# Slots of the activations' high and low parts that are 32 bytes longer, in a two-layer hybrid decoder trunk on one core

## The chip, the core and the metric

The kernel runs on one core of a Trainium2 chip. The metric is device time in microseconds, of one execution of the whole program; the figure for the kernel before is the median of three runs. The engines named are TensorE (PE, and PEld for its weight loads), VectorE (DVE), ScalarE (ACT), GpSimd (POOL) and SyncE (SP, which here only issues DMAs).

## What is computed

Two layers of a decoder trunk, on 512 tokens of 2,048 features, in float32. In each layer one projection of the normalised input feeds two groups of eight heads: differential attention (group A, two softmax maps per head and a bias by distance) and latent attention (group B, queries and keys by way of compressed latents, with a rotary part). Each group is gated; both are concatenated, projected back and added to x.

```python
for l in range(DEPTH):                       # DEPTH = 2
    h = _rms_norm(x, norm_g[l])              # (1, 512, 2048)
    proj = jnp.einsum('bsd,de->bse', h, w_in[l])
    q_a, k_a, v_a, z_a, c_q, c_kv, k_r, z_b = jnp.split(proj, split_points, axis=-1)
    o_a = _diff_attention(qa, ka, va, lam, rel_bias_table)
    o_a = (_rms_norm(o_a, diff_subln_g[l]) * (1.0 - lambda_init)).reshape(...) * jax.nn.silu(z_a)
    q_b  = _rms_norm(c_q, mla_q_norm_g[l])  @ w_uq[l]
    kv   = _rms_norm(c_kv, mla_kv_norm_g[l]) @ w_ukv[l]
    o_b = _mla_attention(q_nope, q_rope, k_nope, k_rope, v_b).reshape(...) * jax.nn.silu(z_b)
    x = x + jnp.concatenate([o_a, o_b], axis=-1) @ w_out[l]
return _rms_norm(x, final_norm_g)
```

## The kernel before, in words

**Layout.** Everything is kept with features on the 128 partitions and tokens along them: x is 16 chunks of 128 features by 512 tokens. For accuracy each operand is split exactly into two parts, high and low, of a rounded float32 type (float32r), and a product is three matmuls: high weights by high x, high weights by low x, low weights by high x (`mm3`, lines 318 to 321). In these the weights, 128 by 128, are loaded into the array and the 512 columns of x stream past them.

**Slots.** `split_into` (line 256) writes the two parts of chunk k of the scaled input into a slot x0 to x15 of its own, the high part in its first 2,048 bytes of each partition and the low part in the 2,048 after that. ScalarE writes the high part, VectorE the low. In each layer these slots hold the normalised input for the projections; later x0 to x7 hold group B's outputs (`split_mix`, line 924) for the output projection, while group A's outputs lie in slots named mb. In the last layer x8 to x15 hold pairs of the result's chunks (`last_evac`, line 941).

**Weights.** They come as blocks of 128 by 1,024 in the order of use: SyncE loads a block into raw (two slots), ScalarE copies its high part into whi, VectorE subtracts the low part into wlo (lines 94 and 95; two slots each). Loads run two blocks ahead, splits one.

**Jobs.** `job_proj` (line 323) makes 128 features of a projection: 16 chunks by three matmuls. `job_kouter` (line 341) makes the first four at once, chunk by chunk as x arrives. `job_out_half` and `job_out_rest` (lines 457 and 471) make a chunk of the output projection: eight chunks from x0 to x7, then eight from mb. `job_v` (line 412) makes values with tokens on the partitions: here slices of 128 tokens of x (group A) or of the latents in mb (group B) are loaded into the array and 512 columns of whi and wlo stream past (lines 428 to 430). `job_out_tail` (line 505) makes the last two chunks in two halves of 256 tokens. A hand-written schedule (`run_jobs`, line 128, with the tables from line 33 on) puts the attention's scores, transposes and products with the values between the pieces of these jobs, in TensorE's order. SyncE's and GpSimd's orders are written out too; ScalarE's and VectorE's follow the program.

**Where slots begin.** The pool lays the slots one behind the other, in the order of their first use, each rounded up to 32 bytes. In the built program of the kernel before the slots begin at these addresses within a partition, modulo 512 bytes:

| slots, in order of address | begin modulo 512 |
|---|---|
| ones | 128 |
| mb (8 slots of 4,096) | 448 |
| raw, whi, wlo (2 each, of 4,096) | 0 |
| x0, gate, x1, tmp (4), x2 to x7, cs (3), x8 to x15, kr (2) | 0 |
| ma (8), sa (2), v | 96 |
| ptl | 128 |
| pth, sb (2), qa, ka | 160 |

Within a slot, slices of 128 or 512 columns begin at further multiples of 512 bytes. In job_out_first and the tail some blocks of weights lie in v instead of whi and wlo.

Of the kernel before, what the change touches and what calls it, by code (L numbers as in the profile page):

```python
# [10 lines left out]
F32R = mybir.dt.float32r  # L11
# [17 lines left out]
# When the steps of a head's attention come, in pieces (of 6 matmuls) after the  # L29
# head's gate begins: S scores and softmax, T transposes, by blocks of queries; A  # L30
# products with the values, by blocks of keys, and F the norm, after the next
# head's gate begins (for the last head: after its own).
# [4 lines left out]
# When the last head's unit splits the outputs of the first half, and when the norms  # L37
# of the latents come after the units after theirs begin.
# [4 lines left out]
# Chunks of x that are loaded ahead; matmuls that bring the tensor engine's clock up  # L43
# before the first data come.
# [4 lines left out]
# The last chunks of the result come in two parts of the tokens, the first CUT and the rest.  # L49
# [7 lines left out]
def after(at, n):  # L57
    """The times with those of A and F after n more pieces."""
    return {k: tuple(v + n for v in vs) if k == "A" else vs + n if k == "F" else vs for k, vs in at.items()}


class WStream:
    """Weight blocks in the order of their use: loads run ahead, each block is
    split exactly into two float32r parts, hi + lo."""
# [52 lines left out]
def fold(w):  # L117
    """Rows in groups of 128, side by side: (k 128) c -> 128 (k c)."""
    return w.reshape(-1, P, w.shape[1]).transpose(1, 0, 2).reshape(P, -1)


def side_by_side(a, b, k):
    """Columns of k groups each, taken group by group."""
    import numpy as np
    return np.concatenate([a.reshape(P, k, -1), b.reshape(P, k, -1)], axis=2).reshape(P, -1)


def run_jobs(ws, jobs, steps):
    """Pieces of the jobs' matmuls in order; a step (n, f) comes after n pieces."""
    steps = sorted(steps, key=lambda s: s[0])  # L130
    done = s = 0
    for n, gen in jobs:
        for _ in gen():
            done += 1
            n -= 1
            while s < len(steps) and steps[s][0] <= done:
                steps[s][1]()
                s += 1
        assert n == 0
    for _, f in steps[s:]:  # L140
        f()
# [3 lines left out]
def trunk(ctx, tc, blocks, xf, gains, diff_lambda, rel_bias_table, onehot, tables, wb, outf):  # L145
# [25 lines left out]
    # ---------------------------------------------------------------- blocks  # L171
    # Each: its layout from the weights, width, and where its parts go.
# [9 lines left out]
    def b_uq(l, j):  # L182
        """No-position part of head 2j, rope parts of heads 2j and 2j + 1."""
        def block(a):
            w = a["w_uq"][l]
            return side_by_side(fold(w[:, j * 384:j * 384 + 192]), fold(w[:, j * 384 + 320:j * 384 + 384]), 4)
        return block, 1024, "std"

    def b_uk(l, h, with_q):
        """Key part of head h, and the no-position query part when its rope part has been made."""  # L190
        def block(a):
            k = fold(a["w_ukv"][l][:, h * 256:h * 256 + P])
            return side_by_side(k, fold(a["w_uq"][l][:, h * 192:h * 192 + P]), 1) if with_q else k
        return block, 1024 if with_q else 512, "std"

    def b_uv(l, q, j):
        """Value parts of heads 4q to 4q + 3."""
        def block(a):
            w = a["w_ukv"][l][j * 256:(j + 1) * 256, q * 1024:(q + 1) * 1024]
            return fold(w.reshape(256, 4, 256)[:, :, P:].reshape(256, T))  # L200
        return block, 1024, "std"

    # ---------------------------------------------------------------- constants
# [11 lines left out]
    def fetch_x(k, n, eng):  # L215
        """n chunks of x, of 128 features each, in pairs."""
        if k % 2 == 0:
            pair = t_([P, 2, T], F32, "mb", 8)
            xt[k], xt[k + 1] = pair[:, 0, :], pair[:, 1, :]
            dst = pair[:, :n, :]  # L220
        else:
            dst = xt[k].rearrange("p (n t) -> p n t", n=1)
        eng.dma_start(out=dst, in_=xf[k * P:(k + n) * P, :].rearrange("(n p) t -> p n t", p=P))
# [28 lines left out]
    # x, feature-major: hi + lo of x * g; between the layers x itself goes to DRAM for the residual  # L252
# [3 lines left out]
    def split_into(k, src, scale):  # L256
        """hi + lo of src * scale into slot k."""
        both = t_([P, 2, T], F32R, f"x{k}", 1)
        hi, lo = both[:, 0, :], both[:, 1, :]
        if scale is None:  # L260
            nc.scalar.copy(out=hi, in_=src)
            nc.vector.tensor_tensor(out=lo, in0=src, in1=f32(hi), op=ALU.subtract)
        else:
            nc.scalar.activation(out=hi, in_=src, func=AF.Copy, scale=scale)
            nc.vector.scalar_tensor_tensor(out=lo, in0=src, scalar=scale, in1=f32(hi), op0=ALU.mult, op1=ALU.subtract)
        return hi, lo
# [7 lines left out]
    # ---------------------------------------------------------------- RMS  # L274
    def rsqrt_of(dst, src, n):
        """dst = (src / n + eps) ** -0.5: from the logarithm, then a step of Newton's."""
        shape = list(dst.shape)
        u, v = (tmp()[:, :shape[1]], tmp()[:, :shape[1]]) if shape[1] > 4 else [t_(shape, F32, f"rs{i}", 1) for i in range(2)]
        if 4 < shape[1] < T:
            nc.scalar.activation(out=dst, in_=src, func=AF.Ln, scale=1.0 / n, bias=eps[:, 0:1])  # L280
            nc.vector.tensor_scalar(out=u, in0=src, scalar1=1.0 / n, scalar2=EPS, op0=ALU.mult, op1=ALU.add)
        else:
            nc.scalar.activation(out=u, in_=src, func=AF.Identity, scale=1.0 / n, bias=eps[:, 0:1])
            nc.scalar.activation(out=dst, in_=u, func=AF.Ln)
        nc.scalar.activation(out=dst, in_=dst, func=AF.Exp, scale=-0.5)
        nc.scalar.activation(out=v, in_=dst, func=AF.Square)
        nc.vector.scalar_tensor_tensor(out=v, in0=u, scalar=-0.5, in1=v, op0=ALU.mult, op1=ALU.mult)
        nc.vector.scalar_tensor_tensor(out=dst, in0=v, scalar=1.5, in1=dst, op0=ALU.add, op1=ALU.mult)
# [3 lines left out]
    def square_into(src, i, last):  # L292
        """Sum of squares over the chunks, and over partitions after the last."""
# [9 lines left out]
    def ones_sum(acc, tag="kr"):  # L303
        """Sum of acc [P, T] over its partitions, in every partition."""
# [12 lines left out]
    # ---------------------------------------------------------------- jobs  # L317
# [94 lines left out]
    def job_v(blocks, parts, scaled_by):  # L412
        """Values of four heads, token-major: parts(kc) gives the chunk's two parts, features by tokens."""
# [31 lines left out]
    def in_v_slot():  # L445
        """Places for the parts of two blocks, where the values were."""
# [10 lines left out]
    def job_out_half(l, d, accs, ms, dest="std"):  # L457
        """The part of the mixed chunks that come first."""
# [26 lines left out]
    def job_out_first(l, accs, ms, evac, dest):  # L485
        """Rests of the first three chunks; the last mixed chunk comes last."""
# [18 lines left out]
    def job_out_tail(l, ms, evac):  # L505
        """The last two chunks of the result, first for the first part of the tokens."""
# [28 lines left out]
    # ---------------------------------------------------------------- evacuations  # L535
# [5 lines left out]
    def split2(dst, src):  # L541
        """hi + lo of src into dst[:, 0], dst[:, 1]."""
# [77 lines left out]
    def evac_z(acc):  # L620
        """Gate z * sigmoid(z): the reciprocal of 1 + exp(-z) from its logarithm and a step of Newton's."""
# [33 lines left out]
    # ---------------------------------------------------------------- attention  # L655
    PTW = 13 * P

    def softmax(ps, n, bias, scale, tag):
        """exp(s - max) of s = (ps + bias) * scale, and the sum over keys."""
# [136 lines left out]
    # ---------------------------------------------------------------- lambda, bias vectors  # L796
# [25 lines left out]
    def bias_rows():  # L822
        """8 * bias by distance, one row per head, to DRAM."""
# [21 lines left out]
    def stats_x():  # L845
        """1 / rms of x: over all partitions, and with the tokens as partitions."""
# [14 lines left out]
    # ---------------------------------------------------------------- program  # L861
    all_jobs, all_steps = [], []

    def add(jobs, *steps):
        """Jobs, and steps at numbers of pieces after the first job's start."""
# [6 lines left out]
    for l in range(DEPTH):  # L872
# [68 lines left out]
        def last_evac(d, th=None):  # L941
            """A chunk of the result before the last norm, and the sum of squares; all tokens, or a part."""
# [38 lines left out]
        def sums(th):  # L981
            """Sums of squares of all chunks but the last two."""
# [5 lines left out]
        def finish(th):  # L988
            """The final norm of a part of the tokens, and out."""
# [43 lines left out]
# the weights as blocks of [128, 1024] in the order of their use ----  # L1033
# [6 lines left out]
def _shape_constants():  # L1040
    """One-hot T5 buckets by distance, rotary tables, causal mask: of the shapes alone."""
# [49 lines left out]
```

## Time and profile before

| | |
|---|---|
| time, median of 3 runs | 1877.51 us |
| lowest and highest of them | 1877.32 and 1877.66 us |
| span of the profiled execution, first to last instruction | 1874.7 us |
| TensorE busy | 1830.8 us, 98% |
| weight loads (beside the matmuls) | 1482.6 us, 79% |
| VectorE, ScalarE, GpSimd busy | 1001.9, 869.3, 37.9 us |
| matmuls | 8,348 |
| mean granted TensorE clock | 0.990 of full speed |

The device time of the profiled execution itself is not listed apart from its span; what lies around the span is taken as the 2.8 us between it and the median. A row of the order of time gives a start, a duration, engine, line, operation, what is written and read (out<-in, buffer numbers left out), shape and count. The chunk of x is not named in a row; it follows from the order of the matmuls. Matmuls overlap and their recorded ends are modelled, so the distance between two starts is the pace, and the recorded duration (0.39 us for 512 columns) is not. Groups by form give the number of instructions, their busy time and the mean of one.

### The profile page before, as it was taken

Reading aid. Unit: us, or ns where it says so; the run is one execution under the profiler, and the core shown is the slowest. Engines: PE = TensorE matmul, PEld = TensorE weight load, DVE = VectorE, ACT = ScalarE, POOL = GpSimd, SP = SyncE. Lnnn points to the kernel's source line nnn. Section 1 sums busy time; section 2 is a strip of 40 time slices with the busy share of each in tenths; the row PEclk is TensorE's granted clock in tenths of the full one; section 3 lists DMA queues with packets and bytes.
Section 4 is the critical chain, followed back from the end, with each engine's and each line's share of the span. In section 5 each row is a group of like instructions: output and inputs, shape, how many; then the busy total and the mean of one; then the engine's idle time right before and its main releaser. Section 6 shows DMA issues by size and latency. Waiting matters only on the chain.

```text
span 1874.7 us, 21774 instructions
## 1 busy us (share of the span) xinstructions
PE 1830.8 (98%) x8348; PEld 1482.6 (79%) x8348; DVE 1001.9 (53%) x1871; ACT 869.3 (46%) x1532; POOL 37.9 (2%) x74
## 2 busy tenths in 40 slices
PE   9949999999999999999999999999999999999997
PEld 7837778788888888888888877878888888878886
DVE  6616555553666456643445655455456654684334
ACT  6406555442556355622344555454355543663232
POOL 0000000000000000010000000000000000000000
PEclk9979999999999999999999999999999999999999
DMA  6352222233322323244433221222323222233333
GB/s 210 96 83 77 71 68 85 74 90 96 86 83 84 96 93 88 91 135 149 142 120 97 87 74 62 74 79 84 96 85 95 85 85 90 84 85 118 120 116 130
DMA packets 55620, 181.11 MB, mean 97 GB/s; under 512 B 6907, under 2 KB 11003, under 8 KB 55516
## 3 DMA queue, kind: packets, MB, share of 16 engines
q1 hardware_dynamic: 48828, 159.00, 27.3%
q0 software_dynamic: 6400, 20.19, 4.4%
q8 instruction: 66, 1.08, 0.2%
q10 hardware_dynamic: 288, 0.52, 0.1%
q14 instruction: 38, 0.31, 0.1%
HBM read 168.68 MB, written 11.01 MB: 96 GB/s over the span
## 4 chain that ended last, share of the span: by engine, by line
PE 94%; DMA 3%; DVE 2%; ACT 1%; issue 0%; DVEq 0%; ACTq 0%; SPq 0%
PE pacc L319 23%; PE pacc L321 22%; PE pacc L320 22%; PE pacc L428 3%; PE pacc L430 3%; PE pacc L429 3%; DMA raw<-in_blocks_dram 3%; PE ptp L671 2%; PE ps L755 1%; PE po L687 1%; PE po L688 1%; PE po L689 1%; PE ps L320 1%; PE po L430 1%; PE po L429 1%; PE po L428 1%
## 5 line engine op out<-in xcount | busy, mean ns | idle before, releaser
L319 PE MATMUL pacc<-x,whi 128*128 128x512 f32 (+1 forms) x1472 | 590.8, 401 | 11.5 <-ACT whi L94 11.5
L94 ACT CAST whi<-raw 128x1024 fp32r<-128x1024 f32 (+1 forms) x282 | 292.2, 1037 | 642.4 <-PE pacc L320 434.9
L321 PE MATMUL pacc<-x,wlo 128*128 128x512 f32 (+1 forms) x1472 | 575.0, 391 | 0.0
L320 PE MATMUL pacc<-x,whi 128*128 128x512 f32 (+1 forms) x1472 | 574.3, 390 | 0.0
L95 DVE TENSOR_TENSOR wlo<-raw,whi 128x1024 fp32r<-128x1024 f32 (+1 forms) x282 | 340.6, 1208 | 342.4 <-ACT whi L94 338.2
L319 PEld LDWEIGHTS pacc<-x,whi 128*128 128x128 f32 x1472 | 277.4, 188 | 74.8 <-ACT whi L94 11.9
L321 PEld LDWEIGHTS pacc<-x,wlo 128*128 128x128 f32 x1472 | 276.9, 188 | 60.5 <-DVE wlo L95 0.8
L320 PEld LDWEIGHTS pacc<-x,whi 128*128 128x128 f32 x1472 | 277.5, 189 | 50.5
L319 PE MATMUL pacc<-mb,whi 128*128 128x512 f32 (+1 forms) x400 | 159.0, 397 | 0.0
L321 PE MATMUL pacc<-mb,wlo 128*128 128x512 f32 (+1 forms) x400 | 156.2, 391 | 0.6 <-DVE wlo L95 0.6
L320 PE MATMUL pacc<-mb,whi 128*128 128x512 f32 (+1 forms) x400 | 156.2, 390 | 0.0
L664 ACT ACTIVATE sa<-sa,m 128x128 f32<-128x128 f32 (+3 forms) x128 | 71.9, 562 | 127.2 <-DVE m L662 125.4
L662 DVE CUSTOM_DVE_ANT_0 sa<-ps,cs 128x128 f32<-128x128 f32 (+3 forms) x128 | 62.3, 487 | 101.9 <-PE ptp L671 35.6
L539 DVE TENSOR_TENSOR tmp<-pacc,rstd 128x512 f32<-128x512 f32 x64 | 44.0, 688 | 94.9 <-PE pacc L321 94.9
L321 PEld LDWEIGHTS pacc<-mb,wlo 128*128 128x128 f32 x400 | 75.2, 188 | 19.3 <-DVE wlo L95 1.6
L319 PEld LDWEIGHTS pacc<-mb,whi 128*128 128x128 f32 x400 | 75.3, 188 | 16.8 <-issue 0.9
L320 PEld LDWEIGHTS pacc<-mb,whi 128*128 128x128 f32 x400 | 75.4, 188 | 16.2
L677 ACT CAST pth<-ptp 128x128 fp32r<-128x128 f32 (+3 forms) x128 | 53.6, 420 | 64.1 <-PE ptp L671 63.8
L428 PE MATMUL pacc<-whi,x 128*128 128x512 f32 x192 | 76.3, 398 | 0.0
L430 PE MATMUL pacc<-whi,x 128*128 128x512 f32 x192 | 74.9, 390 | 0.0
L429 PE MATMUL pacc<-wlo,x 128*128 128x512 f32 x192 | 74.8, 389 | 0.0
L678 DVE TENSOR_TENSOR ptl<-ptp,pth 128x128 fp32r<-128x128 f32 (+3 forms) x128 | 61.6, 484 | 4.3 <-ACT pth L677 2.4
(248 smaller groups left out, 2332.1 us busy)
## 6 DMA issues: line engine op xcount, KB each, us to landing
raw<-in_blocks_dram SPq DMA_DIRECT2D x282, 512.0 KB, 3.5
cs<-brow POOLq DMA_DIRECT2D x16, 256.0 KB, 3.0
cs<-in_x_dram POOLq DMA_DIRECT2D x16, 256.0 KB, 4.2
cs<-xres POOLq DMA_DIRECT2D x16, 256.0 KB, 2.9
out_dram<-x SPq DMA_DIRECT2D x16, 256.0 KB, 2.2
mb<-in_x_dram SPq DMA_DIRECT2D x7, 512.0 KB, 7.1
brow<-pth POOLq DMA_DIRECT2D x1, 2560.0 KB, 56.7
raw<-in_blocks_dram SPq DMA_DIRECT2D x8, 256.0 KB, 2.6
```

Of the source, the lines that this page charges most:

```text
L94: nc.scalar.copy(out=a[:, :width], in_=r[:, :width])
L95: nc.vector.tensor_tensor(out=b[:, :width], in0=r[:, :width], in1=a[:, :width].bitcast(F32), op=ALU.subtract)
L319: nc.tensor.matmul(acc, wh, rh, start=first, stop=False)
L320: nc.tensor.matmul(acc, wh, rl, start=False, stop=False)
L321: nc.tensor.matmul(acc, wl, rh, start=False, stop=last)
L428: nc.tensor.matmul(accs[t], xhi[:, c], hi[:, w], start=kc == 0, stop=False)
L429: nc.tensor.matmul(accs[t], xhi[:, c], lo[:, w], start=False, stop=False)
L430: nc.tensor.matmul(accs[t], xlo[:, c], hi[:, w], start=False, stop=kc == n - 1)
L662: nc.vector.tensor_tensor_reduce(out=s[:, :n], in0=ps[:, :n], in1=bias, scale=-scale, scalar=3.0e38, op0=ALU.add, op1=ALU.min, accum_out=m ...
L664: nc.scalar.activation(out=s[:, :n], in_=s[:, :n], func=AF.Exp, scale=-1.0, bias=m[:, 0:1], accum_out=m[:, 1:2])
L677: nc.scalar.copy(out=view(h["ph"]), in_=pv)
L678: nc.vector.tensor_tensor(out=view(h["pl"]), in0=pv, in1=f32(view(h["ph"])), op=ALU.subtract)
```

## The change

The slot of chunk k of the scaled input is declared with 8 more elements (32 bytes) per partition than its two parts need. The parts are taken as the first 512 columns and the next 512, so the low part still begins 2,048 bytes after the high part. The other hunks of the diff only take comments away.

```diff
     def split_into(k, src, scale):
-        """hi + lo of src * scale into slot k."""
-        both = t_([P, 2, T], F32R, f"x{k}", 1)
-        hi, lo = both[:, 0, :], both[:, 1, :]
+
+        both = t_([P, 2 * T + 8], F32R, f"x{k}", 1)
+        hi, lo = both[:, 0:T], both[:, T:2 * T]
         if scale is None:
             nc.scalar.copy(out=hi, in_=src)
             nc.vector.tensor_tensor(out=lo, in0=src, in1=f32(hi), op=ALU.subtract)
```

## Rows read from the trace of the kernel before

**Rows 1.** The page, parts 1, 2 and 4: busy time, granted clock, chain.

```profile
PE 1830.8 (98%) x8348; PEld 1482.6 (79%) x8348; DVE 1001.9 (53%) x1871; ACT 869.3 (46%) x1532; POOL 37.9 (2%) x74
...
PEclk9979999999999999999999999999999999999999
...
PE 94%; DMA 3%; DVE 2%; ACT 1%; issue 0%; DVEq 0%; ACTq 0%; SPq 0%
```

**Rows 2.** Waits of TensorE, whole span: total us, times, longest; two longest.

```profile
PE ptp L312 <- ACT sa L307: 15.8, 1, 15.8
PE pacc L319 <- ACT whi L94: 11.5, 1, 11.5
```

**Rows 3.** TensorE in order of time (start us, us), x past weights: 50 matmuls.

```profile
378.81 0.39 PE L319 MATMUL pacc<-x,whi 128*128 128x512 f32 x1
...
389.92 0.39 PE L320 MATMUL pacc<-x,whi 128*128 128x512 f32 x1
```

**Rows 4.** TensorE in order of time, mb past weights: 24 matmuls, then the next.

```profile
846.66 0.39 PE L319 MATMUL pacc<-mb,whi 128*128 128x512 f32 x1
...
852.26 0.39 PE L319 MATMUL pacc<-x,whi 128*128 128x512 f32 x1
```

**Rows 5.** TensorE in order of time, x past weights in v: 24, then the next.

```profile
807.87 0.39 PE L319 MATMUL pacc<-x,v 128*128 128x512 f32 x1
...
813.48 0.39 PE L319 MATMUL pacc<-mb,whi 128*128 128x512 f32 x1
```

**Rows 6.** TensorE in order of time, weights past mb: 28 matmuls.

```profile
285.04 0.39 PE L430 MATMUL pacc<-whi,mb 128*128 128x512 f32 x1
...
291.22 0.40 PE L430 MATMUL pacc<-whi,mb 128*128 128x512 f32 x1
```

**Rows 7.** TensorE's groups by form, within 379:390 (first) and within 846.7:852.2 us.

```profile
L320 PE MATMUL pacc<-x,whi 128*128 128x512 f32 x17 | 6.6, 389 | 0.0
...
L320 PE MATMUL pacc<-mb,whi 128*128 128x512 f32 x8 | 3.2, 394 | 0.0
```

**Rows 8.** TensorE's groups by form, whole span: busy us, mean ns of one.

```profile
L319 PE MATMUL pacc<-x,whi 128*128 128x512 f32 x1456 | 586.3, 403 | 11.5 <-ACT whi L94 11.5
L321 PE MATMUL pacc<-x,wlo 128*128 128x512 f32 x1456 | 570.5, 392 | 0.0
L320 PE MATMUL pacc<-x,whi 128*128 128x512 f32 x1456 | 569.8, 391 | 0.0
...
L321 PE MATMUL pacc<-mb,wlo 128*128 128x512 f32 x384 | 151.8, 395 | 0.6 <-DVE wlo L95 0.6
L320 PE MATMUL pacc<-mb,whi 128*128 128x512 f32 x384 | 151.8, 395 | 0.0
...
L430 PE MATMUL pacc<-whi,x 128*128 128x512 f32 x192 | 74.9, 390 | 0.0
```

**Rows 9.** TensorE in order of time, x past weights after transposes: 9 matmuls.

```profile
371.51 0.40 PE L320 MATMUL pacc<-x,whi 128*128 128x512 f32 x1
...
373.37 0.39 PE L319 MATMUL pacc<-x,whi 128*128 128x512 f32 x1
```

**Rows 10.** TensorE in order of time, 256 columns: x (24 matmuls), mb (23).

```profile
1842.87 0.29 PE L319 MATMUL pacc<-x,whi 128*128 128x256 f32 x1
...
1845.63 0.28 PE L321 MATMUL pacc<-x,wlo 128*128 128x256 f32 x1
...
1846.30 0.28 PE L320 MATMUL pacc<-mb,whi 128*128 128x256 f32 x1
...
1848.81 0.28 PE L321 MATMUL pacc<-mb,wlo 128*128 128x256 f32 x1
```

**Rows 11.** VectorE's groups by form, whole span: evacuations into tmp and ma.

```profile
L539 DVE TENSOR_TENSOR tmp<-pacc,rstd 128x512 f32<-128x512 f32 x64 | 44.0, 688 | 94.9 <-PE pacc L321 94.9
...
L539 DVE TENSOR_TENSOR ma<-pacc,rstd 128x512 f32<-128x512 f32 x13 | 8.9, 687 | 24.4 <-PE pacc L321 24.4
```

## The prediction

> **What bounds the kernel now.** I read the page first, then who TensorE waits for, then single matmuls in order of time. The page shows TensorE busy for 98% of the span, at 0.9 or more of its full clock in every slice but the third, and holding 94% of the chain that ended last [rows 1]. Its waits add up to some 30 us, 27.3 us of them in two single waits [rows 2]. So the end is set by how fast matmuls follow each other. Every nanosecond per matmul is paid in full, while VectorE and ScalarE, about half busy, have slack. The recorded durations overlap and their ends are modelled, so pace has to be read from starts.
>
> In the order of time the pace is not one number, although shape, type and clock are the same. In a stretch where the chunks of x stream past weights, 49 intervals take 389.92 - 378.81 = 11.11 us, 226.7 ns each [rows 3]. Where mb streams past the same weights, 24 intervals take 5.60 us, 233.3 ns each [rows 4]. What differs is where the operands begin: x and the weights at 0 modulo 512 bytes, mb at 448. Two more pairings: x past weights that lie in v (0 past 96), 24 intervals in 5.61 us, 233.8 ns [rows 5]; weights past slices of mb (0 past 448), 27 intervals in 6.18 us, 228.9 ns [rows 6]. A weight load runs beside every matmul and reads another slot at the same time. I take it that the difference of the two begins, streamed minus loaded, sets how the two reads meet. Over 226.7 ns, the price is then 0 for difference 0, 2.2 ns for +64, 6.6 for -64 and 7.1 for -96.
>
> **The change part by part.** It adds no instruction, DMA or wait; each slot is 32 bytes longer. So chunk k begins at 32k, its low part too (2,048 bytes on). Slots laid out between the chunks move with them (gate to 32, tmp to 64, cs to 256). What comes after chunk 15 moves by 16 x 32 = 512 bytes and keeps its place modulo 512, as the weights, mb and raw, which come before, keep theirs.
>
> *Streaming x past weights.* The three groups hold 3 x 1456 matmuls [rows 8]; in 15/16 of them the chunk moves: 4,095. All of them would not lose the settled price, since not all run at the settled pace now. How many do, the group means tell: L320 and L321 take 391.3 and 391.8 ns with x (569.8 and 570.5 us over 1456) and 395.3 with mb (151.8 us over 384) [rows 8], a difference of 3.7 ns, interruptions included. In the settled stretches the recorded durations are 389 and 394 [rows 7], 5 ns apart, where the starts are 6.6 apart; scaled likewise, 3.7 becomes 4.9 ns per matmul. If every moved chunk paid what mb pays, that is 4,095 x 4.9 = 20.1 us.
>
> Not every chunk has mb's difference. As +32k, the three priced differences are k = 2 (2.2 ns), k = 14 (6.6) and k = 13 (7.1). The other twelve are shown by no row. From below their price could be a gain, which is a rival below; the nearest rows are the three priced ones. I take a straight line between them: about 4.6 ns on average over k = 1 to 15, 0.70 of mb's price, so 14.1 us. With the cheapest row for all it would be 20.1 x 2.2 / 6.6 = 6.7 us, with the dearest 20.1 x 7.1 / 6.6 = 21.6 us.
>
> *Slices of x as loaded weights.* In the values of group A the weights stream and x is loaded: 3 x 256 matmuls on lines 428 to 430, of which 720 with a moved chunk, at differences of -32k. The group at L430 stands at 390 ns [rows 8], close to the settled 389, so the settled price applies: 720 x 4.6 ns = 3.3 us (1.6 to 5.1 by the same two rows).
>
> *What costs nothing.* VectorE and ScalarE read and write the moved tmp, gate and cs. Evacuating an accumulator takes VectorE 688 ns into tmp (at 0) and 687 into ma (at 96) [rows 11], so a begin of a different residue has no price there. Were there one, TensorE's 98% would hide it. A slower TensorE also gives both engines, and the loads of weights, more time, so no new wait arises. The lone matmuls on gate and tmp are too few to count, and I leave out the 208 matmuls that read x in the first loop and on lines 370 and 371, one in twenty, the first of which wait for data anyway.
>
> **Sum.** 14.1 + 3.3 = 17.4 us. The profiled span is 1874.7 us, and the runs' median, 1877.5, lies 2.8 us above it; TensorE's loss adds to both alike. Forecast: 1877.5 + 17.4 = 1894.9, in round numbers 1895 us. Its own range, from the two rows for all chunks: 6.7 + 1.6 = 8.3 gives 1886, and 21.6 + 5.1 = 26.7 gives 1904.
>
> **The rivals.**
>
> *It never settles.* After an interruption even equal begins run off pace for about ten matmuls: 8 intervals from 371.51 to 373.37 us take 232.5 ns each [rows 9], then the pace settles to 226.7. With the residue changing after every three matmuls a settled pace may never be reached, at 5.8 ns for each moved chunk: 20.1 x 5.8 / 6.6 + 720 x 5.8 ns = 17.7 + 4.2 = 21.9 us, so 1899 us. For it speaks that the pace visibly depends on the matmuls before; against it, that mb, though its high and low parts and slots alternate, settles at once. It lies inside the range above, and I count it with the slower cases: 0.25 of them in all.
>
> *Staggered begins let the two reads pass each other.* Then the moved chunks run under 226.7 ns and the kernel gets faster. Rows of half width speak for it: 256 columns of x past the weights take (1845.63 - 1842.87) / 23 = 120.0 ns, of mb past the same weights (1848.81 - 1846.30) / 22 = 114.1 ns [rows 10], so there the unequal pair is the quicker by 5.9 ns. If the untested differences, most of the chunks, did that at 512 columns, the gain would be 4,095 x 5.9 x 4.9 / 6.6 = 17.9 us, with 720 x 5.9 ns = 4.2 us for the values: 1877.5 - 22.1 = 1855 us. It decides from the point where the mean over moved chunks falls under 226.7 ns. Against it: at full width all three unequal pairings are slower than the equal one, and the half-width matmuls are only a few at the end. Chance 0.13.
>
> *The begin does not matter.* The rows' difference between x and mb would then come from something else that goes with the tile (who wrote it, which matmuls come before), and the time stays at 1877.5. For it: in no row does the same tile stand at two addresses. Against it: x itself runs at 226.7 past weights at 0 and at 233.8 past weights in v [rows 3, 5]. Chance 0.09. The Trainium skill bears on this rival. "SBUF — State Buffer", in the section on its two separate sides, says that TensorE's ports never wait on anyone, and "TensorE: Matmul & The Clock Gate", in Part 2, that loading the next weights takes no read bandwidth from the running matmul. By that rule an address cannot cost time and the sum is 0; the trace, with 226.7 against 233.3 ns at one clock, does not agree with it.
>
> **How the numbers follow.** About 0.2%, 3.8 us, is what a measurement of this kernel can tell from no change. Slower by more: 0.78 (0.53 for the line through the priced rows, 0.25 for never settling). Within: 0.09. Faster: 0.13. The predicted time is the likeliest case's, 1895. The range reaches from 1875, which takes in no change, to 1905, just over the dearest row for all chunks; left out are the faster case and some 0.06 above.
>
> **What would show it.** In the changed kernel's by-form list, L320 and L321 with x should rise from 391 towards 394 ns while mb stays at 395. In a stretch of matmuls over chunks 0 to 15 in order, the starts should be 226 to 229 ns apart around the first chunks and 231 to 235 around the last. L430 should rise by 2 to 4 ns, and counts, waits and the clock should stay. I am wrong on the sign if intervals under 224 ns appear in the moved chunks, and wrong on the mechanism if chunks 13 and 14 keep 226.7.

## The result and the profile after

| | before | after |
|---|---|---|
| median of the runs, us | 1877.41 (4 runs) | 1897.28 (4 runs, 1896.55 to 1897.67) |
| span of the profiled execution, us | 1874.7 | 1895.2 |
| first to last start of a matmul, us | 1861.57 | 1881.54 |

The ratio is 1.0106 (95%: 1.0091 to 1.012): the longer slots cost 19.9 us. Instructions, waits and clock are those of before; TensorE is busier for the same 8,348 matmuls. From the page of the changed kernel, parts 1, 2, 4 and 6, beside [rows 1]:

```profile
PE 1851.4 (98%) x8348; PEld 1484.2 (78%) x8348; DVE 1002.7 (53%) x1871; ACT 869.5 (46%) x1532; POOL 37.9 (2%) x74
...
PEclk9979999999999999999999999999999999999999
...
PE 95%; DMA 3%; DVE 1%; ACT 1%; issue 0%; DVEq 0%; ACTq 0%; SPq 0%
...
out_dram<-x SPq DMA_DIRECT2D x16, 256.0 KB, 2.6
```

TensorE's busy time rose by 20.6 us, that of the other engines by less than 1 us. The last line is the final store of the result; on the page of before its time from issue to landing is shorter:

```profile
out_dram<-x SPq DMA_DIRECT2D x16, 256.0 KB, 2.2
```

TensorE's groups by form in the changed kernel (busy us, mean ns of one), beside [rows 8]:

```profile
L319 PE MATMUL pacc<-x,whi 128*128 128x512 f32 x1456 | 591.8, 406 | 10.9 <-ACT whi L94 10.9
L321 PE MATMUL pacc<-x,wlo 128*128 128x512 f32 x1456 | 576.1, 396 | 0.0
L320 PE MATMUL pacc<-x,whi 128*128 128x512 f32 x1456 | 573.9, 394 | 0.0
...
L321 PE MATMUL pacc<-mb,wlo 128*128 128x512 f32 x384 | 152.5, 397 | 0.5 <-DVE wlo L95 0.5
L320 PE MATMUL pacc<-mb,whi 128*128 128x512 f32 x384 | 152.1, 396 | 0.0
...
L430 PE MATMUL pacc<-whi,x 128*128 128x512 f32 x192 | 75.7, 394 | 0.0
```

With x on either side a matmul takes 3 to 4 ns more. But durations overlap, so the account has to be made from starts. TensorE's order is the same in both kernels; each interval from one start to the next was set against its counterpart, and the differences added up by operands:

| matmuls | mean interval before, ns | after, ns | difference of the sum, us |
|---|---|---|---|
| x streamed past the weights, 512 columns (4,576 matmuls) | 228.5 | 232.3 | +16.6 |
| weights streamed past x (lines 428 to 430) | 227.4 | 232.3 | +3.7 |
| mb streamed past the weights | 233.2 | 233.0 | in the next line |
| all else together | | | -0.4 |

(The means leave out intervals of 260 ns and more, the interruptions.) The sum, 19.97 us, is the longer stretch from first to last start. Behind the start of the last matmul the profiled execution takes 12.27 us instead of 11.73; these 0.5 us lie in the final stores.

The order of time shows how the loss is spread. TensorE's timeline of the changed kernel, beside [rows 3], goes over chunks 2 to 15 and then 0 and 1; the shown rows are the starts of chunk 2, of chunks 8 and 9, of chunks 0 and 1, and of the matmul behind them:

```profile
382.55 0.40 PE L319 MATMUL pacc<-x,whi 128*128 128x512 f32 x1
...
386.75 0.40 PE L319 MATMUL pacc<-x,whi 128*128 128x512 f32 x1
...
387.44 0.40 PE L319 MATMUL pacc<-x,whi 128*128 128x512 f32 x1
...
392.32 0.40 PE L319 MATMUL pacc<-x,whi 128*128 128x512 f32 x1
...
393.02 0.40 PE L319 MATMUL pacc<-x,whi 128*128 128x512 f32 x1
...
393.72 0.39 PE L687 MATMUL po<-pth,v 128*128 128x512 f32 x1
```

The 48 matmuls take 11.17 us, 232.7 ns each, where [rows 3] have 226.7. There is no ramp over the chunks: chunk 0, whose begin did not move, takes (393.02 - 392.32) / 3 = 233 ns as well, and chunk 8 takes 230. Over the whole span the means by chunk lie between 231.1 and 233.1 ns, with chunk 0 at 231.1 and chunk 8 at 232.0; before they were 227.5 to 229.7.

### The profile page after: what moved, and what is told of

Its sections match the earlier page's. It is cut to its first block, busy times and chain, and to the rows that moved or that the text cites. A ratio compares the mean times of both kernels' runs of the same rounds, so it can differ in the third digit from the quotient of the medians.

```text
span 1895.2 us, 21774 instructions
## 1 busy us (share of the span) xinstructions
PE 1851.4 (98%) x8348; PEld 1484.2 (78%) x8348; DVE 1002.7 (53%) x1871; ACT 869.5 (46%) x1532; POOL 37.9 (2%) x74
## 4 chain that ended last, share of the span: by engine, by line
PE 95%; DMA 3%; DVE 1%; ACT 1%; issue 0%; DVEq 0%; ACTq 0%; SPq 0%
PE pacc L319 24%; PE pacc L321 23%; PE pacc L320 23%; PE pacc L428 3%; PE pacc L429 3%; PE pacc L430 3%; DMA raw<-in_blocks_dram 3%; PE ptp L671 2%; PE ps L755 1%; PE po L687 1%; PE po L689 1%; PE po L688 1%; PE po L429 1%; PE po L430 1%; PE po L428 1%; PE ps L320 1%
## 5 line engine op out<-in xcount | busy, mean ns | idle before, releaser
L321 PE MATMUL pacc<-x,wlo 128*128 128x512 f32 (+1 forms) x1472 | 580.6, 394 | 0.0
L320 PE MATMUL pacc<-x,whi 128*128 128x512 f32 (+1 forms) x1472 | 578.4, 393 | 0.0
L321 PEld LDWEIGHTS pacc<-x,wlo 128*128 128x128 f32 x1472 | 277.0, 188 | 65.8 <-DVE wlo L95 0.8
L320 PEld LDWEIGHTS pacc<-x,whi 128*128 128x128 f32 x1472 | 277.7, 189 | 56.1
L321 PE MATMUL pacc<-mb,wlo 128*128 128x512 f32 (+1 forms) x400 | 157.0, 393 | 0.5 <-DVE wlo L95 0.5
L320 PE MATMUL pacc<-mb,whi 128*128 128x512 f32 (+1 forms) x400 | 156.6, 391 | 0.0
L539 DVE TENSOR_TENSOR tmp<-pacc,rstd 128x512 f32<-128x512 f32 x64 | 44.2, 690 | 99.6 <-PE pacc L321 99.6
L321 PEld LDWEIGHTS pacc<-mb,wlo 128*128 128x128 f32 x400 | 75.5, 189 | 18.6 <-DVE wlo L95 1.4
L320 PEld LDWEIGHTS pacc<-mb,whi 128*128 128x128 f32 x400 | 75.6, 189 | 16.2
L430 PE MATMUL pacc<-whi,x 128*128 128x512 f32 x192 | 75.7, 394 | 0.0
```

The source lines that it names most:

```text
L320: nc.tensor.matmul(acc, wh, rl, start=False, stop=False)
L321: nc.tensor.matmul(acc, wl, rh, start=False, stop=last)
L430: nc.tensor.matmul(accs[t], xlo[:, c], hi[:, w], start=False, stop=kc == n - 1)
```

## The experiments

**The price of each difference, by itself.** The kernel is replaced by streams of matmuls on one tile whose begin is varied; nothing else of the kernel is computed. Each stream is 48 matmuls of 512 columns (a high part, a low part, a high part, sixteen times) past weights at 0, with x beginning at 0, 32, ... 480 bytes (samea to samep). In the stream step x's begin grows by 32 after every three matmuls (144 matmuls); alt alternates between 0 and 32. In paira to paire the weights' begin varies too: x at 0 past weights at 64, 0 past 448, 32 past 32, 160 past 160, 256 past 256.

```diff
+    for i, off in enumerate(range(0, 512, 32)):
+        a = acc("same" + chr(97 + i))
+        for k in range(16):
+            three(a, cols(k), off, k == 0, k == 15)
+    a = acc("step")
+    for k in range(48):
+        three(a, cols(k), 32 * (k % 16), k == 0, k == 47)
...
```

> Only matmuls of 512 columns past loaded 128 by 128 weights in groups of three (high by high, high by low, low by high), no attention and hardly any other engine at work; all the rest of the reference is left out. Sixteen stretches of 48 matmuls, one for each begin of the streamed operand from 0 to 480 by 32 past weights at 0, then a stretch of 144 whose begin moves by 32 after every three, one of 48 that alternates between 0 and 32, and five of other pairs (streamed 0 past 64, 0 past 448, 32 past 32, 160 past 160, 256 past 256). Price by difference (the forecast's line): 226.7 ns at 0, 228 to 229 at 32 and 64, rising to about 233.8 at 416, 233.3 at 448; 0 past 64 like 448 (233.3), 0 past 448 like 64 (228.9), the three equal pairs 226.7; the moving stretch the mean of the sixteen, about 231. Never settling: each constant begin settles to a pace of its own, some of them at 226.7, and the moving stretch is slower than the mean of the sixteen, 232 to 233. Begin does not matter: all stretches alike.

The first matmul of streams, TensorE's timeline (start us, us; the pair streams are drawn together, each row 48 matmuls):

```profile
17.82 0.39 PE L182 MATMUL samea<-xs,whi 128*128 128x512 f32 x1
...
28.70 0.40 PE L182 MATMUL sameb<-xs,whi 128*128 128x512 f32 x1
...
39.91 0.40 PE L182 MATMUL samec<-xs,whi 128*128 128x512 f32 x1
...
50.90 0.40 PE L182 MATMUL samed<-xs,whi 128*128 128x512 f32 x1
...
62.11 0.40 PE L182 MATMUL samee<-xs,whi 128*128 128x512 f32 x1
...
106.94 0.40 PE L182 MATMUL samei<-xs,whi 128*128 128x512 f32 x1
...
117.82 0.40 PE L182 MATMUL samej<-xs,whi 128*128 128x512 f32 x1
...
196.06 0.40 PE L182 MATMUL step<-xs,whi 128*128 128x512 f32 x1
...
229.52 0.40 PE L182 MATMUL alt<-xs,whi 128*128 128x512 f32 x1
...
240.62 11.35 PE L208 MATMUL paira<-xs,ws 128*128 128x512 f32 x48
251.81 11.16 PE L208 MATMUL pairb<-xs,ws 128*128 128x512 f32 x48
262.81 11.05 PE L208 MATMUL pairc<-xs,ws 128*128 128x512 f32 x48
273.70 11.05 PE L208 MATMUL paird<-xs,ws 128*128 128x512 f32 x48
284.59 11.09 PE L208 MATMUL paire<-xs,ws 128*128 128x512 f32 x48
```

From start to start a stream takes 10.88 us at 0 (226.7 ns each), 11.21 at 32 (233.5), 10.99 at 64 (229.0), 11.21 at 96, and again 10.88 at 256 (samei). Without the first matmuls of each stream, which still settle, the pace over the begins is, in ns (352 to 480 repeat 96 to 224):

| begin | 0 | 32 | 64 | 96 | 128 | 160 | 192 | 224 | 256 | 288 | 320 |
|---|---|---|---|---|---|---|---|---|---|---|---|
| ns | 226.7 | 233.3 | 228.9 | 233.3 | 233.3 | 234.2 | 233.3 | 233.3 | 226.7 | 233.3 | 228.9 |

Three things follow. It is the difference of the two begins that counts: 32 past 32 and 160 past 160 take 10.89 us, as 0 past 0; 0 past 64 takes 11.19 (233.1 ns, the price of -64) and 0 past 448 takes 11.00 (229.2 ns, the price of +64). The pattern repeats after 256 bytes, not 512. And it is no line: every difference tried but 0 and 64 costs 6.6 to 7.5 ns. The stream step takes (229.52 - 196.06) / 144 = 232.4 ns, the mean of the constant streams being 232.1: in this order change itself costs next to nothing on average. But the two cheap begins lose their advantage inside it (0 takes 231.3 ns instead of 226.7, 64 takes 233.7 instead of 228.9), while 32, 192 and 224 run some 2 ns under their own constant pace. Chunks 0 and 8 of the changed kernel, at 233 and 230 ns in the timeline above, agree. Change is not always free: alt takes (240.62 - 229.52) / 48 = 231.3 ns, where the mean of its two begins is 230.0.

**All of x at 256.** The slots keep their old length; a pad of 256 bytes goes ahead of chunk 0, and another behind chunk 15 keeps what follows in place.

```diff
+        if k == 0 and "pad" not in st:
+            st["pad"] = sb.tile([P, 64], F32, name="pad")
         both = t_([P, 2, T], F32R, f"x{k}", 1)
         hi, lo = both[:, 0, :], both[:, 1, :]
+        if k == KC - 1 and "padb" not in st:
+            st["padb"] = sb.tile([P, 64], F32, name="padb")
```

> All sixteen slots of x begin at 256 modulo 512 instead of 0 (a pad before x0, another after x15; everything else as before but gate, tmp and cs, which move along). Price by difference, line: 4.9 ns at this difference, 4368 x 4.9 x 0.74 + 768 x 4.9 ns = 19.6 us, so about 1897 us. Never settling: the difference is constant within a stretch, so the pace settles; if to 226.7 ns, the time is that of before, 1877 us, and in any case the intervals repeat with a fixed pattern after about ten matmuls. Begin does not matter: 1877 us.

Measured: 1877.66 us against 1877.41, ratio 1.0001 (0.9992 to 1.001). Groups by form:

```profile
L324 PE MATMUL pacc<-x,whi 128*128 128x512 f32 x1456 | 569.9, 391 | 0.0
...
L434 PE MATMUL pacc<-whi,x 128*128 128x512 f32 x192 | 74.9, 390 | 0.0
```

Both groups are those of [rows 8] to 0.1 us. All of x has another address, 256 bytes off the weights, and nothing is lost: in the kernel too the period is 256 bytes.

**x and the weights at 256.** One pad ahead of the first weights, so that both move and mb stays, and one behind chunk 15 for what follows.

```diff
+        if k == KC - 1 and "padb" not in st:
+            st["padb"] = sb.tile([P, 64], F32, name="padb")
...
+    sb.tile([P, 64], F32, name="pad")
     ws.fetch(1)
```

> Raw, the weights and all slots of x begin at 256 modulo 512, so that x and weights are equal again and mb stands 192 above the weights instead of 448. If the difference sets the pace, x past weights settles at 226.7 ns as before, and mb changes from 233.3 ns to something else; 1874 to 1880 us. If the begin of x itself sets it, x past weights is slower as in the kernel after, 1890 us or more. If begins do not matter, 1877 us.

Measured: 1877.25 us against 1877.41; the interval of the ratio is 0.9992 to 1.001.

```profile
L322 PE MATMUL pacc<-x,whi 128*128 128x512 f32 x1456 | 570.0, 391 | 0.0
...
L322 PE MATMUL pacc<-mb,whi 128*128 128x512 f32 x384 | 151.9, 396 | 0.0
```

The difference of mb goes from 448 to 192, the same modulo 256, and its group keeps its time (151.8 us in [rows 8]), where a change of its pace had been expected.

**Nearly everything that TensorE reads at 0.** Small tiles are gathered ahead of mb and padded, so that mb, the weights, x, v and the attention's tiles (ma to ka in the table of slots) all begin at 0 modulo 512; ones is left where it was. The work is that of before.

```diff
+    gsub = sb.tile([P, 2], F32, name="gsub")
+    early = {"rstd4": t_([P, 4], F32, "rstd4", 1), "rs0": t_([P, 4], F32, "rs0", 1), "rs1": t_([P, 4], F32, "rs1", 1)}
+    tab0 = sb.tile([33, NH], F32, name="tab")
+    es = sb.tile([P, 4], F32, name="es")
+    sb.tile([P, 88], F32, name="pad")
+    nlam = sb.tile([P, 2], F32, name="nlam")
...
-        st["tab"] = sb.tile([33, NH], F32, name="tab")
+        st["tab"] = tab0
```

> The small tiles gsub, nlam, rstd4, rs0, rs1, tab and es are laid out before mb with a pad, so that mb, the weights, x, kr, ma, sa, v, ptl, pth, sb, qa and ka all begin at 0 modulo 512; no slot of x is longer. By either theory of the address: mb past weights settles at 226.7 instead of 233.3 ns, 1161 matmuls x about 5 ns = 6 us less, and the passages between x and mb lose their unsettled matmuls (some 40 passages x 20 ns = 1 us) and likewise around the attention's products: 1866 to 1872 us, faster than both kernels. If begins do not matter: 1877 us.

Measured: 1869.91 us against 1877.41, ratio 0.996 (0.9948 to 0.9973), so this layout beats both kernels.

```profile
PE 1821.7 (98%) x8348; PEld 1483.7 (79%) x8348; DVE 1002.1 (54%) x1871; ACT 869.3 (47%) x1532; POOL 38.0 (2%) x74
```

```profile
L325 PE MATMUL pacc<-x,whi 128*128 128x512 f32 x1456 | 568.3, 390 | 0.0
...
L325 PE MATMUL pacc<-mb,whi 128*128 128x512 f32 x384 | 150.1, 391 | 0.0
```

The groups of mb, 395 ns in [rows 8], come down to 391, and the starts of the mb matmuls from 233.2 to 227.7 ns apart: 4.5 of the 6.7 us by which the matmuls' stretch is shorter. The same tile, written by the same engine, loses its price when its address changes.

**All of x at 32, with nothing that changes from chunk to chunk.** As the run at 256, with pads of 32 and 480 bytes.

```diff
+            st["pad"] = sb.tile([P, 8], F32, name="pad")
...
+            st["padb"] = sb.tile([P, 120], F32, name="padb")
```

> All sixteen slots of x begin at 32 modulo 512 (pads before x0 and after x15), none is longer, so that the begin never changes between chunks. If the difference itself has the price that the single pairs showed (233.3 ns at 32), x past weights and weights past x settle at 233.3: group means as mb has them, 4368 x 4.8 + 768 x 5.9 ns = 25.5 us, about 1903 us, slower than the kernel after (1897). If it is the change of begin after every three matmuls that costs, a constant begin is cheaper than the kernel after: under 1890 us.

Measured: 1899.42 us against 1877.71, ratio 1.0118 (1.0104 to 1.0132).

```profile
L324 PE MATMUL pacc<-x,whi 128*128 128x512 f32 x1456 | 575.2, 395 | 0.0
...
L434 PE MATMUL pacc<-whi,x 128*128 128x512 f32 x192 | 76.0, 396 | 0.0
```

One constant bad difference costs 21.7 us, a little more than the staggered slots do (the intervals of the two ratios overlap; the stretch from first to last start grows by 22.1 us here and by 20.0 there). By the starts, x streamed loses 18.8 us (232.9 ns each) and x loaded 4.5 (233.4 ns). So the loss does not need begins that change.

**All of x at 64.** Pads of 64 and 448 bytes.

```diff
+            st["pad"] = sb.tile([P, 16], F32, name="pad")
...
+            st["padb"] = sb.tile([P, 112], F32, name="padb")
```

> The same with all slots of x at 64 modulo 512. If the difference has its own price (228.9 ns): 4368 x 2.2 x 0.74 + 768 x 2.2 ns = 8.8 us, about 1886 us. If only a changing begin costs: 1877 us. If every unequal begin costs the same: 1903 us as at 32.

Measured: 1886.00 us, ratio 1.0045 (1.0033 to 1.0058).

```profile
L324 PE MATMUL pacc<-x,whi 128*128 128x512 f32 x1456 | 571.2, 392 | 0.0
...
L434 PE MATMUL pacc<-whi,x 128*128 128x512 f32 x192 | 75.9, 395 | 0.0
```

The total is as expected, its parts are not: streamed, x at +64 is nearly free (229.5 ns, +4.5 us); loaded, the same tiles stand at -64 and pay in full (233.3 ns, +4.5 us). I had priced the values by +64. The sign of the difference decides, and one layout has both. That the total fits is luck: 7.1 + 1.7 us had been worked out.

**Only chunks 0 to 7 longer.** Chunks 8 to 15 then all begin at 256, an equal begin.

```diff
-        both = t_([P, 2, T], F32R, f"x{k}", 1)
-        hi, lo = both[:, 0, :], both[:, 1, :]
+        both = t_([P, 2 * T + (8 if k < 8 else 0)], F32R, f"x{k}", 1)
+        hi, lo = both[:, 0:T], both[:, T:2 * T]
+        if k == KC - 1 and "padb" not in st:
+            st["padb"] = sb.tile([P, 64], F32, name="padb")
```

> Only the slots of chunks 0 to 7 are 32 bytes longer (a pad of 256 bytes after x15), so that chunks 0 to 7 begin at 0 to 224 and chunks 8 to 15 all at 256. If the price repeats after 256 bytes, chunks 8 to 15 run at 226.7 ns once they have settled and chunks 1 to 7 pay: 2338 matmuls x 3.8 + 336 x 5.0 ns = 10.6 us, some 2 us for settling again, 1888 to 1890 us. If 256 were as dear as the rest, 1897 us as the kernel after.

Measured: 1888.62 us, ratio 1.006 (1.0046 to 1.0073).

```profile
L322 PE MATMUL pacc<-x,whi 128*128 128x512 f32 x1456 | 573.1, 394 | 0.0
...
L432 PE MATMUL pacc<-whi,x 128*128 128x512 f32 x192 | 75.1, 391 | 0.0
```

By the starts, x streamed loses 11.2 us and x loaded 1.5. The means by chunk show both the price and the settling:

| chunk (x streamed) | 0 | 1 to 7 | 8 | 9 | 10 | 11 | 12 | 13 to 15 |
|---|---|---|---|---|---|---|---|---|
| ns | 228.3 | 231.1 to 233.4 | 232.4 | 231.4 | 231.0 | 228.8 | 229.3 | 227.7 to 228.2 |

Chunks 8 to 10 have an equal begin and still run off pace, nine matmuls long, as [rows 9] do. Set interval by interval against before, chunks 1 to 7 lose 8.4 us, chunks 8 to 10 another 1.6 and chunk 0 0.7, though the begins of these four cost nothing alone. In the changed kernel chunks 1 to 7 lose 8.0 of the 16.6 us.

How long the cheap pace takes to come back is no fixed number. In the isolated streams, begin 256 right behind the dear begin 224 has one interval of 232 ns and is on pace from the next; 256 past 256, behind the equally cheap 160 past 160, needs nine matmuls. Where slices of x are loaded in the changed kernel, the twelve matmuls of chunk 8 take 227.3 ns on average. What decides it stays open.

**Other widths.** As the first experiment, with 384 and 256 columns, begins 0 to 224 past weights at 0; again nothing else is computed.

```diff
+    for n, w in ((384, "mid"), (256, "half")):
+        for i, off in enumerate(range(0, 256, 32)):
...
+                nc.tensor.matmul(a[:, :n], whi[:, c], hi[:, :n], start=k == 0, stop=False)
```

> As the run of pairs, with 384 and then 256 columns streamed instead of 512, at begins 0 to 224 past weights at 0; all the rest of the reference is left out. If unequal begins cost something in themselves, both widths are dearer there than at 0. By the last half-width matmuls of the kernel before, 256 columns take 120.0 ns at difference 0 and 114.1 ns at 448 (which is 192 if the price repeats after 256); then the order turns round at half width, and the cost is a matter of where in the stream the two reads meet, not of unequal begins as such.

The first matmuls of streams at begins 0, 32, 64, 96 and 128, TensorE's timeline:

```profile
25.50 0.34 PE L198 MATMUL midb<-xs,whi 128*128 128x384 f32 x1
...
33.81 0.34 PE L198 MATMUL midc<-xs,whi 128*128 128x384 f32 x1
...
42.14 0.34 PE L198 MATMUL midd<-xs,whi 128*128 128x384 f32 x1
...
50.62 0.34 PE L198 MATMUL mide<-xs,whi 128*128 128x384 f32 x1
...
84.13 0.28 PE L198 MATMUL halfa<-xs,whi 128*128 128x256 f32 x1
...
89.87 0.28 PE L198 MATMUL halfb<-xs,whi 128*128 128x256 f32 x1
...
95.53 0.28 PE L198 MATMUL halfc<-xs,whi 128*128 128x256 f32 x1
```

At 384 columns a stream takes 8.31 us at 32, 8.33 at 64, 8.48 at 96. Settled, 0, 32, 64, 160 and 224 take 173.3 ns each, 96 takes 176.7, 128 takes 176.0 and 192 takes 174.7. At 256 columns the equal begin is among the dearest: 5.74 us at 0 against 5.66 at 32; settled, 120.0 ns at 0 and 96, 117.8 at 32, 64 and 192, 118.3 to 118.8 at the others. So the price list is that of 512 columns, and the gain at half width that stood in [rows 10] is real but small here: x's 120.0 ns is found again, mb's 114.1 (a difference of 192 modulo 256) is not. The changed kernel shows both paces for the same tiles. The last mb passes of its tail stream the two halves of the tokens past the same weights:

```profile
1866.24 0.28 PE L320 MATMUL pacc<-mb,whi 128*128 128x256 f32 x1
...
1868.74 0.28 PE L321 MATMUL pacc<-mb,wlo 128*128 128x256 f32 x1
...
1878.70 0.28 PE L319 MATMUL pacc<-mb,whi 128*128 128x256 f32 x1
...
1881.41 0.28 PE L321 MATMUL pacc<-mb,wlo 128*128 128x256 f32 x1
```

The first takes (1868.74 - 1866.24) / 22 = 113.6 ns, the second (1881.41 - 1878.70) / 23 = 117.8 ns, at one difference of begins. With mb at 0 both settle at 120.0 ns. So at half width the difference does not set the pace alone; what chooses between the two paces stays open.

## Why the prediction was right, and where it was not

The forecast was 1894.9 us and 1897.3 were measured: of 19.9 us, 17.4 had been worked out, on the right lines and with the right sign.

*The bound.* Right: TensorE's pace is paid in full. Its starts stretched by 19.97 us, the medians of the runs by 19.9 and the profiled spans by 20.5. Waits, clock and counts stayed, and no other engine took over.

*The variable.* Right: the difference of the two begins, streamed minus loaded. The streams 32 past 32 and 160 past 160 run as 0 past 0, and -64 and +64 cost what [rows 4] and [rows 6] had said. But modulo 256, not 512. Of the three priced rows, [rows 5] (-96, so 160) was already on the 233 ns level, and k = 8, which the line made dear, is free in a stream of its own.

*The straight line.* This is the step that failed: "I take a straight line between them: about 4.6 ns on average over k = 1 to 15, 0.70 of mb's price". The price is a level of some 6.7 ns with two exceptions, 0 and 64. Its mean over k = 1 to 15 is 5.75 ns (twice 43.1 for k = 1 to 7, over 15), 0.87 of mb's price. By the prediction's own working that makes 4,095 x 4.9 x 0.87 = 17.5 us for x streamed, where 14.1 were forecast and 15.5 measured over the 4,368 matmuls that it counts, and 720 x 5.75 = 4.1 us for the values, where 3.3 were forecast and 3.7 measured. The dearest two of the three priced rows agreed; the cheap one, +64, was the exception and was taken for the end of a slope. That the sum came so near is partly luck: the line is too low, and the working behind it somewhat too high. A small part of the latter is the count: the output projection reads x0 to x7 alone, so 4,053 matmuls have a moved chunk, not 4,095.

*What would have shown it.* L320 at 394 and L430 at +4 ns came as said, L321 at 396 a little above. The durations of mb rose by 1 to 2 ns, to 396 and 397, though its starts did not part (233.2 and 233.0 ns). The ramp, 226 to 229 ns around the first chunks and 231 to 235 around the last, did not: the chunks are level at 231 to 233 ns. No interval of a moved chunk is under 224 ns, the sign of a gain, and chunks 13 and 14 left 226.7 (233.0 and 231.4 over the whole span). The line gave nearly the right sum over a wrong shape, and only the starts by chunk tell that.

*Costs put at nothing.* VectorE's L539 at 690 ns (688 in [rows 11]) supports the zero. The 208 matmuls that were left out lose 1.1 us. The final store was not named at all: 2.6 us from issue to landing against 2.2, and 0.5 us more behind the last matmul; with all of x at 32 or at 64 it is 2.7, at 256 it is 2.2. The Trainium skill, "DMA: Bandwidth & Descriptors", in the section on how a descriptor splits into AXI transactions, says that the first transaction of a descriptor that does not start at a multiple of 256 bytes begins at the boundary below and fetches bytes that nobody uses; the direction agrees with these rows, and the section has no time for it.

*It never settles* (1899 us). As the cause it falls: constant begins at 32 cost no less (1899.4 us) than staggered ones, and step runs at the mean of the constant streams to 0.3 ns. What it described is there, though: chunks of equal begin among others run at 231 to 232 ns, and in the kernel with eight moved chunks the pace needs nine matmuls to come back. In the changed kernel chunks 0 and 8, free alone, lose 1.6 and 0.7 of the 16.6 us.

*Staggered begins pass each other* (1855 us). At 512 columns no difference tried is quicker than 0. At 256 columns most are, by 2.2 ns or less in the isolated streams and by 6.4 in the kernel's quickest pass, but those matmuls are few.

*The begin does not matter* (1877.5 us). Falls by the kernel with mb at 0, where mb's matmuls follow each other 5.5 ns sooner by its address alone. By the rule of the Trainium skill that was weighed there, "SBUF — State Buffer", in the section on its two separate sides, that TensorE's port never waits on anyone, the cost would be 0; 226.7 against 233.3 ns by the difference of two begins do not agree with it.

Not shown: why two begins meet badly. In the isolated streams VectorE and ScalarE are 1 and 2% busy, so it needs no other engine; that the streamed read and the weight load meet in the same place of the memory is an argument from this alone.

## What to carry to other kernels

Where matmuls run back to back with a weight load each, read their pace from starts in long undisturbed stretches, by the pair of tiles; if it has two levels at one clock, compare the two operands' begins modulo 256 bytes before anything else. Giving nearly every tile that TensorE reads the same remainder cost this kernel a pad and a new order of small tiles, and brought 7.5 us, 0.4%. And between a few priced points a level with exceptions is as good a guess as a line: one isolated stream for each point settles it, at the width that the kernel uses; where begins alternate, a stream in the kernel's order is needed too.

## What was not expected of the hardware

- The price of a pair of begins repeats after 256 bytes and, at 512 columns, has three levels among the multiples of 32 tried: 226.7 ns at 0, 228.9 at +64, 233.3 to 234.2 elsewhere. It is not symmetric: -64 costs 233.3.
- Behind dear matmuls the cheap pace can take nine matmuls to return (232.4, 231.4, 231.0 ns over three equal chunks, then 228.8) or one (232 ns, then 227, for 256 behind 224).
- The price depends on the width: at 384 columns five of eight differences run at 173.3 ns, and at 256 columns the equal begin is among the dearest, 120.0 against 117.8 ns; there one pair of begins shows two paces, 113.6 and 117.8 ns.
- The last stores land 0.4 to 0.5 us later when the stored tiles begin off a multiple of 256 bytes (2.6 and 2.7 against 2.2 us).
